# Layer sums accumulated by TensorE through an identity product, and casts of the recurrent mixer moved from VectorE to ScalarE and GpSimd

## The chip, the core and the metric

The kernel runs on one core of one Trainium2 chip. Its engines are TensorE (PE; PEld is its weight load), VectorE (DVE), ScalarE (ACT), GpSimd (POOL) and SyncE (SP), which here only issues DMAs. The metric is the device time of one execution in microseconds (us), as the median of several runs.

## The reference

512 tokens of width 1024 go through two layers. In each layer `x = LN(alpha*x + mixer(x))` and then `x = LN(alpha*x + MoE(x))`. Layer 0 has a convolution mixer, layer 1 a recurrent mixer (RG-LRU). The mixture of experts sends each token to 2 of 16 experts.

```python
def rglru_mixer(x, ...):
    y_branch, xr = split(x @ w_in)
    xr = causal_depthwise_conv(xr, c_dw) + c_dw_b
    r = sigmoid(xh @ w_gate_a + b_gate_a)        # xh: xr in 4 heads of 256
    i = sigmoid(xh @ w_gate_x + b_gate_x)
    log_a = -8 * r * softplus(-lam);  a = exp(log_a)
    b = sqrt(-expm1(2 * log_a)) * (i * xr)
    h = scan(h = a * h + b)                      # over the 512 tokens
    return (gelu(y_branch) * h) @ w_out

def moe(x, ...):
    e_idx, gates = route(x)                      # 2 experts of 16 for each token
    y = expert(x[tokens of e]); out[token] += gate * y

for layer in range(2):
    x = layer_norm(alpha * x + mixer(x), ln1_g, ln1_b)
    f = moe(x, ...)
    x = layer_norm(alpha * x + f, ln2_g, ln2_b)
```

All inputs are float32. The kernel splits an operand of most products into a high part (rounded to the fast float32r form) and a low part (what is left) and makes three products of them: high x high, high x low, low x high.

## The kernel before

Each engine runs its instructions strictly in the order in which the program's text issues them; nothing is reordered, and an instruction that waits holds up all behind it on its engine. So the order of the calls in the Python text is the order of the work.

**Weights.** `Stream` loads pieces of weights by SP's DMA queue, in a planned list. `split` makes the high part `wh` on ACT (line 137) and the low part `wl` by a subtraction on DVE or POOL (line 148, `lower`; `low()` sets which engines take turns). `lead` is how many pieces are split ahead of the one in use. With `later = []` the subtractions are put off and cut into quarters, until `lows()` issues them.

**Layer end.** The last expert's product ends in the sum `alpha*x + MoE(x)`. While the last expert (e = 15) runs, `base_begin` loads, by POOL's DMA queue, four tiles `az` (128 tokens of the layer's input, 128x1024) and `ay` (the two expert rows of each token, gathered in DRAM so far), and POOL adds the two rows (line 1491, in tile order 0 to 3). `base_sum(t)` on DVE makes `az = alpha*az + ay` (line 1496). The last expert's output comes in two column halves: `share(h)` scales it by the gate into `yh` (ACT, line 1502) and `yl` (DVE, 1503), `total_mm` puts its rows at their tokens by products with a 0/1 matrix `place` (PE, 1509), and `total_half` adds that to `az` (DVE, 1516) and takes statistics of the sum (DVE `bn_stats`, 1517), 128x512 at a time, 8 times in a layer. After that `moments` (POOL raises to a power, 549) and the normalisation on ACT (1676 in layer 0, 1768 in layer 1) follow. In the same stretch run the last expert's own steps: `turn` transposes the hidden rows and splits them (`ht0h`, `ht1h` on ACT, 418; `ht0l`, `ht1l` on DVE, 421), and `w2(0)` to `w2(3)` are four groups of 12 products; `w2(1)` needs `ht1l` and `w2(3)` is the second half's last. On DVE four quarters of a put-off subtraction (148, 128x512 each) stand between `ht0l` and `ht1l`.

**Recurrent mixer.** `order1` sets its items: x0 to x7 (projections of 128 channels each, with the convolution), g0 to g3 (gates of two x items each), y0 to y7 (gelu branch), a0, i0, a1, i1 (gate weights), o (rows of w_out). An x item is: 24 products on PE, `xc` (ACT, 994), three steps of the convolution on DVE (997, reading a PSUM bank), then the split `xch` of `xc` into high (DVE cast, 420) and low part (DVE subtraction, 421). A g item is 24 products of `xch`, four sigmoids and two tanh on ACT (973, 977), two square roots (983) and products on POOL (978, 984). `spend` puts pieces of the recurrence between the items on DVE (925, 927, 930 to 932). A y item ends in `gy` (ACT, 1007). `finish(c)` multiplies `gy` by the recurrence's result (DVE, 938) and splits the product into `mixo` (DVE cast 420 and subtraction 421) for the output projection (line 651), which starts after y7. The weight piece of y7 is split by ACT right after the `gy` of y6.

Of the kernel before, what the change touches and what calls it, by code (L numbers as in the profile page):

```python
# [11 lines left out]
F32 = mybir.dt.float32  # L12
# [3 lines left out]
AF = mybir.ActivationFunctionType  # L16
OP = mybir.AluOpType
AX = mybir.AxisListType

P = 128  # L20
T = 512
NT = T // P
# [7 lines left out]
ALPHA = 4.0 ** 0.25  # L30
# [317 lines left out]
class Trunk:  # L348
# [564 lines left out]
    def rglru_mixer(self, xT, first, wa, prm, hook):  # L913
        nc, ws, v, lsc = self.nc, self.ws, self.nc.vector, self.lsc
# [21 lines left out]
        def finish(c):  # L936
            y = ys.pop(c)
            v.tensor_tensor(y, y, hs.pop(c), op=OP.mult)
            m = self.V([P, 2, T], F32R, "mixo")
            self.hilo(m[:, 0], m[:, 1], y, False)  # L940
            self.mixo[c] = m

        credit = [0.0]
# [44 lines left out]
        for pos, item in enumerate(self.order1):  # L988
            kind, n = item[0], int(item[1:] or 0)
            hook(item)  # L990
            if kind == "x":
                ps = first.pop(0) if first else self.project_in(xT, ws.get())
                x = self.W([P, T], F32, "xc")
                nc.scalar.activation(x, ps, AF.Identity, bias=prm[:, n, B_C:B_C + 1],
                                     scale=prm[:, n, W_C + 3:W_C + 4])
                for s in range(1, 4):
                    v.scalar_tensor_tensor(x[:, s:], ps[:, 0:T - s], prm[:, n, W_C + 3 - s:W_C + 4 - s],
                                           x[:, s:], op0=OP.mult, op1=OP.add)
                xc[n] = x
                m = self.V([P, 2, T], F32R, "xch")  # L1000
                self.hilo(m[:, 0], m[:, 1], x, False)
                xch[n] = (m[:, 0], m[:, 1])
                spend(1.5)
            elif kind == "y":
                ps = self.project_in(xT, ws.get())
                y = self.W([P, T], F32, "gy")
                nc.scalar.activation(y, ps, AF.Gelu_apprx_tanh)
                ys[n] = y
                spend(4.0)
            elif kind in "ai":  # L1010
                if item != "a0":
                    wg.setdefault(n, []).append(ws.get())
            elif kind == "g":
                gates(n)
                if n % 2:
                    wg.pop(n // 2)
                spend(3.0)
            else:
                self.out_weights(1)
# [331 lines left out]
    def moe(self, layer, loaded):  # L1351

        nc, tc, ws = self.nc, self.tc, self.ws
# [33 lines left out]
        for e in range(E):  # L1387
            cur, last = nxt, e == E - 1
            if e < 12:
                q = e // 4 * 4 + 4 + 2 * (e % 4)  # L1390
                if e % 4 < 2:
                    hot += [self.one_hot(self.pos[:, :, i], nc.gpsimd, i in SMALL) for i in (q, q + 1)]
                if e % 4 == 2:
                    q = e // 4 * 4 + 4
# [21 lines left out]
                    xe = self.gather(slots[e + 2], e + 2 in SMALL, rows)  # L1416
            ws.later = []
            cur.w3(3)
            cur.turn(0)
            ws.lows()  # L1420
            if last:
# [4 lines left out]
            cur.w2(0)  # L1426
            if last:
                loaded()
                self.base_sum(0)
            cur.w2(1)  # L1430
            if e == E - 2:
                self.place_rows(slots[E - 1][0])
# [12 lines left out]
                    self.kept = None  # L1445
        gate = slots[E - 1][1]
        self.share(0, cur.ys[0], gate)
        for t in (1, 2):
            self.base_sum(t)
        ws.lead = 1  # L1450
        cur.w2(2)
        self.base_sum(3)
        ws.lead = 0
        for t in range(NT):
            self.total_mm(t, 0)
        cur.w2(3)
        for t in range(2):
            self.total_half(t, 0)
        self.share(1, cur.ys[1], gate)
        for t in range(2):  # L1460
            self.total_mm(t, 1)
        for t in range(2, NT):
            self.total_half(t, 0)
            self.total_mm(t, 1)
        ws.total, ws.open, ws.cap = False, False, 10
        ws.lead = 4
        ws.later = []
# [12 lines left out]
    def base_begin(self):  # L1480

        nc = self.nc
        self.bz, self.bp, self.yhl, self.bst = [], {}, {}, {}
        for t in range(NT):
            z = self.V([P, D], F32, "az")
            nc.gpsimd.dma_start(z, self.x1d[t * P:(t + 1) * P])  # L1486
            y = self.V8([P, 2, D], F32, "ay")
            nc.gpsimd.dma_start(y, self.yd[2 * t * P:2 * (t + 1) * P].rearrange("(p k) d -> p k d", k=2))  # L1488
            self.bz.append((z, y))
        for _, y in self.bz:  # L1490
            nc.gpsimd.tensor_tensor(y[:, 0], y[:, 0], y[:, 1], op=OP.add)

    def base_sum(self, t):

# [4 lines left out]
    def share(self, h, ps, gate):  # L1499
# [3 lines left out]
        self.nc.vector.scalar_tensor_tensor(lo, ps, gate, hi.bitcast(F32), op0=OP.mult, op1=OP.subtract)  # L1503
        self.yhl[h] = (hi, lo)

    def total_mm(self, t, h):
        ps = self.bp[t, h] = self.bank()
        for i, q in enumerate(self.yhl[h]):
            self.nc.tensor.matmul(ps, self.place[:, t * P:(t + 1) * P], q, start=(i == 0), stop=(i == 1))  # L1509

    def total_half(self, t, h):

        if h == 0:
            self.bst[t] = self.S([P, 2, 6], F32, "bst", bufs=4)
        z = self.halves(self.bz[t])[h]
        self.nc.vector.tensor_tensor(z, z, self.bp.pop((t, h)), op=OP.add)  # L1516
        self.nc.vector.bn_stats(self.bst[t][:, h], z)  # L1517

    def total(self, t):

        self.total_half(t, 1)
        return self.halves(self.bz[t]), self.moments(self.bst.pop(t))

    def extra(self, layer, it):

# [277 lines left out]
```

## Time and profile before

| | us |
|---|---|
| median of 3 runs (1524.83 to 1527.47) | 1525.57 |
| the profiled execution, its own time | 1530.19 |
| its span, first to last instruction | 1528.4 |
| mixture of experts of layer 0 (215 to 700 us) | 485 |
| layer end 0 (700 to 750) | 50 |
| recurrent mixer up to its last input projection (750 to 895) | 145 |
| its output projection, router (895 to 975) | 80 |
| mixture of experts of layer 1 (975 to 1455) | 480 |
| layer end 1 and the output (1455 to 1528) | 73 |

Times in the trace are from the span's start. A timeline row has the start, the length and the instruction, and in brackets how long its engine had been idle and what ended that. A length runs from the start to the end, waiting for a busy resource included; rows that follow on one engine overlap a little. "x4" is four instructions merged.

### The profile page before, as it was taken

The page shows a single profiled execution, that of the slowest core. Times are in us where ns is not written, and L with a number is a line of the kernel's source. Part 1 is how long each engine was busy: PE and PEld are TensorE (multiplying, and loading weights), DVE is VectorE, ACT ScalarE, POOL GpSimd, SP SyncE. Part 2 cuts the span into 40 slices and gives each one's busy share as a digit, 9 for nine tenths or more (in the row PEclk, how much of TensorE's full clock was granted, in tenths as well). Part 3 has the DMA queues.
Part 4 walks back from the last instruction along what each step waited for, and adds up shares of the span by engine and source line. Part 5 has one row for each costly group of instructions (what it writes and reads, how often), then busy time and mean ns, then how long its engine had stood idle before and what let it go on. Part 6 is the DMA issues. An engine that isn't in the chain of part 4 may idle for free. (4 is left out here: it accounts for less than half of the span.)

```text
span 1528.4 us, 18167 instructions
## 1 busy us (share of the span) xinstructions
PE 1396.3 (91%) x6456; PEld 1026.4 (67%) x6456; DVE 1126.9 (74%) x1242; ACT 772.2 (51%) x718; POOL 432.9 (28%) x370
## 2 busy tenths in 40 slices
PE   8999959999999999999689798699999999999972
PEld 7877738677586775677577677485776858665851
DVE  6997788668484774478989987885866748554886
ACT  3543227466473755376546421373755747554741
POOL 3983015204202400003384312250051015000043
PEclk9999979999999999999799999799999999999995
DMA  9645748999999999988823258399999999999771
GB/s 282 219 193 193 286 186 310 392 419 417 420 415 413 421 414 420 420 355 330 228 70 93 94 206 318 144 365 406 421 419 420 410 416 421 415 420 419 286 311 55
DMA packets 120837, 490.71 MB, mean 321 GB/s; under 512 B 14078, under 2 KB 53502, under 8 KB 70564
## 3 DMA queue, kind: packets, MB, share of 16 engines
q1 hardware_dynamic: 102240, 437.29, 72.6%
q0 software_dynamic: 11808, 35.28, 5.9%
q10 hardware_dynamic: 6692, 16.91, 3.0%
q8 instruction: 53, 0.87, 0.2%
q14 instruction: 44, 0.36, 0.1%
HBM read 469.50 MB, written 29.62 MB: 327 GB/s over the span
## 5 line engine op out<-in xcount | busy, mean ns | idle before, releaser
L148 DVE TENSOR_TENSOR wl<-raw,wh 128x2048 fp32r<-128x2048 f32 (+2 forms) x310 | 630.1, 2075 | 242.0 <-ACT wh L137 210.4
L137 ACT ACTIVATE wh<-raw 128x2048 fp32r<-128x2048 f32 (+1 forms) x312 | 535.2, 1757 | 110.3 <-PE p L305 27.0
L305 PE MATMUL p<-wh,xe 128*128 128x512 f32 x1344 | 347.6, 396 | 1.0 <-PEq L1439 0.8
L305 PEld LDWEIGHTS p<-wh,xe 128*128 128x128 f32 x1344 | 248.8, 189 | 56.9 <-issue 7.0
L305 PE MATMUL p<-wl,xe 128*128 128x512 f32 x672 | 187.9, 391 | 3.5 <-DVE wl L148 3.5
L1346 POOL DMA_INDIRECT yd<-y,io x30 | 30.8, 1026 | 497.1 <-ACT y L1344 199.3
L305 PEld LDWEIGHTS p<-wl,xe 128*128 128x128 f32 x672 | 126.0, 188 | 32.3 <-DVE wl L148 5.2
L226 PE MATMUL b<-raw,xs 128*64 128x512 f32 x640 | 146.2, 598 | 0.0
L1278 POOL TENSOR_SCALAR S<-c,posp 128x128 bf16<-128x128 bf16 x96 | 127.0, 1337 | 0.5
L596 PE MATMUL b<-xT,wh 128*128 128x512 f32 (+1 forms) x320 | 119.2, 379 | 6.0 <-ACT wh L137 6.0
L597 PE MATMUL b<-xT,wh 128*128 128x512 f32 (+1 forms) x320 | 118.5, 377 | 3.0 <-DVE xT L421 3.0
L1331 POOL DMA_INDIRECT xe<-x1d,ii x32 | 37.3, 1167 | 291.9 <-PE b L271 138.4
L226 PEld LDWEIGHTS b<-raw,xs 128*64 128x64 f32 x640 | 42.4, 136 | 75.0 <-issue 69.6
L148 POOL TENSOR_TENSOR wl<-raw,wh 128x1024 fp32r<-128x1024 f32 x28 | 71.3, 2555 | 29.3 <-ACT wh L137 14.9
L599 PE MATMUL b<-xT,wl 128*128 128x512 f32 (+1 forms) x320 | 73.5, 373 | 3.8 <-DVE wl L148 3.8
L596 PEld LDWEIGHTS b<-xT,wh 128*128 128x128 f32 x320 | 62.3, 195 | 17.7 <-ACT wh L137 7.6
L597 PEld LDWEIGHTS b<-xT,wh 128*128 128x128 f32 x320 | 62.2, 194 | 13.8 <-DVE xT L421 3.6
L226 PE MATMUL b<-raw,hts 128*64 128x512 f32 x320 | 70.9, 595 | 0.0
L599 PEld LDWEIGHTS b<-xT,wl 128*128 128x128 f32 x320 | 56.9, 191 | 14.3 <-DVE wl L148 4.2
L1344 ACT ACTIVATE y<-p,sg 128x512 f32<-128x512 f32 x40 | 25.3, 685 | 75.4 <-PE p L305 75.4
L761 DVE SCALAR_TENSOR_TENSOR b<-av,c,b 128x510 f32<-128x510 f32 (+27 forms) x87 | 59.8, 731 | 2.2 <-ACT b L754 1.3
L326 DVE TENSOR_TENSOR hs<-hs,p 128x512 f32<-128x512 f32 x44 | 30.2, 685 | 39.6 <-PE p L305 39.6
(309 smaller groups left out, 1913.4 us busy)
## 6 DMA issues: line engine op xcount, KB each, us to landing
raw<-in_moe_w_dram SPq DMA_DIRECT2D x384, 1024.0 KB, 15.3
raw<-in_even_w_in_dram SPq DMA_DIRECT2D x20, 512.0 KB, 7.5
yd<-zero ACTq DMA_DIRECT2D x8, 1024.0 KB, 5.0
ay<-yd POOLq DMA_DIRECT2D x8, 1024.0 KB, 15.0
raw<-in_odd_w_in_dram SPq DMA_DIRECT2D x16, 512.0 KB, 7.5
raw<-in_even_w_out_dram SPq DMA_DIRECT2D x8, 512.0 KB, 8.5
x1d<-z POOLq DMA_DIRECT2D x8, 512.0 KB, 7.6
az<-x1d POOLq DMA_DIRECT2D x8, 512.0 KB, 12.2
```

The lines of the kernel that those rows point to most:

```text
L137: self.k.nc.scalar.activation(wh, raw, AF.Copy)
L148: self.lo[0].tensor_tensor(wl, raw, wh.bitcast(F32), op=OP.subtract)
L226: self.nc.tensor.matmul(ps[64 * h:64 * h + 64], stat[i], w[0][:, i, h * HALF:(h + 1) * HALF], start=(first and i == 0), stop=(last and i = ...
L305: self.nc.tensor.matmul(pss[j], stat[i][a], q[:, i, j * HALF:(j + 1) * HALF], start=(first and i == 0 and a == 0 and q is wh), stop=(last ...
L326: self.nc.vector.tensor_tensor(self.hm[h], self.hm[h], self.p3[h], op=OP.mult)
L596: nc.tensor.matmul(ps, ah, bh, start=(i == 0), stop=False)
L597: nc.tensor.matmul(ps, ah, bl, start=False, stop=False)
L599: nc.tensor.matmul(ps, al, bh, start=False, stop=(i == n - 1))
L761: nc.vector.scalar_tensor_tensor(o[:, s:], av[:, 0:T - s], prm[:, i, 30 - s:31 - s], acc[:, s:], op0=OP.mult, op1=OP.add)
L1278: (eng or self.nc.vector).tensor_scalar(S[:, t], self.iota2 if small else self.iota, pos[:, t:t + 1], None, op0=OP.is_equal)
L1331: self.nc.gpsimd.indirect_dma_start(out=xe, out_offset=None, in_=self.by_half(self.x1d) if small else self.x1d[:, :], in_offset=bass.Indir ...
L1346: nc.gpsimd.indirect_dma_start(out=self.by_half(self.yd) if small else self.yd[:, :], out_offset=bass.IndirectOffsetOnAxis(ap=slot[2], axi ...
```

## The change

It has two parts.

**Layer end.** `base_begin` only loads. A new `base_add`, called after `w3(3)` of the last expert, scales `az` of tiles 0 and 1 by alpha on ACT, and POOL adds the two rows of each tile and, for tiles 0 and 1, also the scaled `az` to that. DVE keeps `base_sum` for tiles 2 and 3. `base_mm` puts `az` into a PSUM bank by a product with the identity (8 in a layer, both operands float32), `total_mm` adds the last expert's rows into the same bank, and `bn_stats` and the normalisation read the bank. The 8 additions on DVE are gone.

**Recurrent mixer.** The high part of `xch` (8 times) and of `mixo` (8 times) is made on ACT, and the low part of `mixo` on POOL.

```diff
@@ finish
-            self.hilo(m[:, 0], m[:, 1], y, False)
+            nc.scalar.activation(m[:, 0], y, AF.Copy)
+            nc.gpsimd.tensor_tensor(m[:, 1], y, m[:, 0].bitcast(F32), op=OP.subtract)
@@ x items
-                self.hilo(m[:, 0], m[:, 1], x, False)
+                self.hilo(m[:, 0], m[:, 1], x)
@@ moe, last expert
             cur.w3(3)
+            if last:
+                self.base_add()
             cur.turn(0)
...
                 loaded()
-                self.base_sum(0)
             cur.w2(1)
...
         self.share(0, cur.ys[0], gate)
-        for t in (1, 2):
-            self.base_sum(t)
         ws.lead = 1
         cur.w2(2)
+        ws.lead = 0
+        for t in range(2):
+            for h in range(2):
+                self.base_mm(t, h)
+        self.base_sum(2)
+        cur.w2(3)
         self.base_sum(3)
-        ws.lead = 0
-        for t in range(NT):
+        self.base_mm(2, 0)
+        self.base_mm(2, 1)
+        for t in range(3):
             self.total_mm(t, 0)
-        cur.w2(3)
-        for t in range(2):
-            self.total_half(t, 0)
+        self.base_mm(3, 0)
+        self.total_mm(3, 0)
         self.share(1, cur.ys[1], gate)
-        for t in range(2):
-            self.total_mm(t, 1)
-        for t in range(2, NT):
-            self.total_half(t, 0)
-            self.total_mm(t, 1)
+        self.total_mm(0, 1)
+        self.total_mm(1, 1)
+        self.base_mm(3, 1)
+        self.total_mm(2, 1)
+        self.total_mm(3, 1)
@@ new and changed functions
+    def base_add(self):
+        nc = self.nc
+        for z, _ in self.bz[:2]:
+            nc.scalar.activation(z, z, AF.Copy, scale=ALPHA)
+        for t, (z, y) in enumerate(self.bz):
             nc.gpsimd.tensor_tensor(y[:, 0], y[:, 0], y[:, 1], op=OP.add)
+            if t < 2:
+                nc.gpsimd.tensor_tensor(z, z, y[:, 0], op=OP.add)
+                self.bz[t] = z
+    def base_mm(self, t, h):
+        ps = self.bp[t, h] = self.bank()
+        self.nc.tensor.matmul(ps, self.ident, self.halves(self.bz[t])[h], start=True, stop=False)
     def total_mm(self, t, h):
-        ps = self.bp[t, h] = self.bank()
+        ps = self.bp[t, h]
         for i, q in enumerate(self.yhl[h]):
-            self.nc.tensor.matmul(ps, self.place[:, t * P:(t + 1) * P], q, start=(i == 0), stop=(i == 1))
+            self.nc.tensor.matmul(ps, self.place[:, t * P:(t + 1) * P], q, start=False, stop=(i == 1))
-        z = self.halves(self.bz[t])[h]
-        self.nc.vector.tensor_tensor(z, z, self.bp.pop((t, h)), op=OP.add)
-        self.nc.vector.bn_stats(self.bst[t][:, h], z)
+        self.nc.vector.bn_stats(self.bst[t][:, h], ps)
     def total(self, t):
-        self.total_half(t, 1)
-        return self.halves(self.bz[t]), self.moments(self.bst.pop(t))
+        return [self.bp.pop((t, h)) for h in range(2)], self.moments(self.bst.pop(t))
```

POOL at layer end 0, behind the loads, before the change:

```order
L1488 DMA ay_5763<-yd_773 128x2048
L1491 TENSOR_TENSOR ay_5753<-ay_5753 128x1024
L1491 TENSOR_TENSOR ay_5756<-ay_5756 128x1024
L1491 TENSOR_TENSOR ay_5760<-ay_5760 128x1024
L1491 TENSOR_TENSOR ay_5763<-ay_5763 128x1024
```

And with the change:

```order
L1494 DMA ay_5763<-yd_773 128x2048
L1503 TENSOR_TENSOR ay_5753<-ay_5753 128x1024
L1505 TENSOR_TENSOR az_5751<-az_5751,ay_5753 128x1024
L1503 TENSOR_TENSOR ay_5756<-ay_5756 128x1024
L1505 TENSOR_TENSOR az_5751<-az_5751,ay_5756 128x1024
L1503 TENSOR_TENSOR ay_5760<-ay_5760 128x1024
L1503 TENSOR_TENSOR ay_5763<-ay_5763 128x1024
```

POOL has six additions in place of four, and the two new ones stand between the others.

DVE at the same place with the change, from the low parts of the turned rows on:

```order
L421 TENSOR_TENSOR ht0l_5878<-b_5872,ht0h_5877 128x512
L148 TENSOR_TENSOR wl_5845<-raw_5769,wh_5844 128x512 x4
L421 TENSOR_TENSOR ht1l_5891<-b_5885,ht1h_5890 128x512
L148 TENSOR_TENSOR wl_5897<-raw_5793,wh_5896 128x2048
L148 TENSOR_TENSOR wl_5916<-raw_5811,wh_5915 128x2048
L1518 SCALAR_TENSOR_TENSOR yl_5935<-p_5894,sg_4361,yh_5934 128x512
L1511 SCALAR_TENSOR_TENSOR az_5758<-az_5758,ay_5760 128x1024
L1511 SCALAR_TENSOR_TENSOR az_5758<-az_5758,ay_5763 128x1024
```

The four quarters still stand ahead of `ht1l`; of the four sums of 128x1024 two are left, both behind `yl`.

ACT at the end of the mixer's input projections (`gy` of y4 to y7, and `wh` pieces), before the change:

```order
L1007 ACTIVATE gy_6924<-b_6899 128x512
L137 ACTIVATE wh_6936<-raw_6626 128x1024 x2
L1007 ACTIVATE gy_6970<-b_6945 128x512
L137 ACTIVATE wh_6976<-raw_6728 128x1024
L1007 ACTIVATE gy_7005<-b_6980 128x512
L137 ACTIVATE wh_6976<-raw_6728 128x1024
L137 ACTIVATE wh_7019<-raw_6890 128x1024
L1007 ACTIVATE gy_7048<-b_7023 128x512
```

And with the change; the second row of `wh_6978` is the weight piece of y7:

```order
L1008 ACTIVATE gy_6926<-b_6901 128x512
L940 ACTIVATE mixo_6929<-gy_6926 128x512
L137 ACTIVATE wh_6938<-raw_6628 128x1024 x2
L1008 ACTIVATE gy_6972<-b_6947 128x512
L940 ACTIVATE mixo_6929<-gy_6972 128x512
L137 ACTIVATE wh_6978<-raw_6730 128x1024
L1008 ACTIVATE gy_7007<-b_6982 128x512
L940 ACTIVATE mixo_7014<-gy_7007 128x512
L137 ACTIVATE wh_6978<-raw_6730 128x1024
L137 ACTIVATE wh_7021<-raw_6892 128x1024
L1008 ACTIVATE gy_7050<-b_7025 128x512
L940 ACTIVATE mixo_7014<-gy_7050 128x512
```

A cast of `mixo`, which needs DVE's multiplication of line 938, now stands ahead of each weight piece: that of channel block 6 ahead of the piece of y7.

## Rows read from the trace of the kernel before

**Rows 1.** Busy time of each engine by stretch (start:end, length, then busy us and instruction counts of PE, PEld, DVE, ACT, POOL; granted TensorE clock as a share of 2.4 GHz; DMA share; GB/s).

```profile
215.00:700.00 485.00, 479.71 (x2211) 333.66 (x2210) 331.20 (x282) 283.57 (x226) 97.22 (x79) 1.00 0.95 387
700.00:750.00 50.00, 36.91 (x146) 28.03 (x144) 46.10 (x50) 23.07 (x23) 20.02 (x18) 0.87 1.06 349
750.00:895.00 145.00, 122.50 (x548) 100.95 (x549) 135.16 (x133) 75.68 (x99) 74.75 (x39) 0.93 0.25 79
...
1455.00:1528.00 73.00, 34.03 (x127) 25.91 (x125) 54.36 (x57) 20.79 (x20) 31.01 (x24) 0.75 0.45 177
```

**Rows 2.** Timeline of POOL, then of DVE, early in the mixer (start, length, instruction); the last row is the same cast with POOL idle.

```profile
770.24 2.42 POOL L1717 TENSOR_TENSOR n<-n,g 128x1024 f32<-128x1024 f32 x1
772.74 2.46 POOL L1718 TENSOR_TENSOR n<-n,b 128x1024 f32<-128x1024 f32 x1
...
768.32 2.32 DVE L997 SCALAR_TENSOR_TENSOR xc<-b,c,xc 128x511 f32<-128x511 f32 x3 [3.80 <-ACT xc L994]
770.73 2.22 DVE L420 CAST xch<-xc 128x512 fp32r<-128x512 f32 x1
772.99 2.77 DVE L421 TENSOR_TENSOR xch<-xc,xch 128x512 fp32r<-128x512 f32 x1
...
790.96 0.43 DVE L420 CAST xch<-xc 128x512 fp32r<-128x512 f32 x1
```

**Rows 3.** Timeline of layer end 0: POOL's additions, DVE, PE's first product that waits for `yl`, ACT's first normalisation, and POOL's first work of the next stage.

```profile
712.69 2.53 POOL L1491 TENSOR_TENSOR ay<-ay 128x1024 f32<-128x1024 f32 x1 [5.28 <-DMA ay<-yd]
717.95 2.45 POOL L1491 TENSOR_TENSOR ay<-ay 128x1024 f32<-128x1024 f32 x1 [2.73 <-DMA ay<-yd]
...
727.38 2.88 POOL L1491 TENSOR_TENSOR ay<-ay 128x1024 f32<-128x1024 f32 x1 [1.49 <-DMA ay<-yd]
...
715.66 2.49 DVE L148 TENSOR_TENSOR wl<-raw,wh 128x512 fp32r<-128x512 f32 x4
718.06 0.68 DVE L421 TENSOR_TENSOR ht1l<-b,ht1h 128x512 fp32r<-128x512 f32 x1
...
728.76 0.79 PE L1509 MATMUL b<-yl,place 128*128 128x512 f32 x1 [4.71 <-DVE yl L1503]
...
743.39 1.52 ACT L1676 ACTIVATE n<-az,mv 128x512 f32<-128x512 f32 x2 [3.30 <-DVE mv L1673]
...
747.48 9.76 POOL L148 TENSOR_TENSOR wl<-raw,wh 128x1024 fp32r<-128x1024 f32 x4
```

**Rows 4.** Timeline of layer end 1: POOL's additions of tiles 0, 1 and 2, DVE's quarters and `ht1l`, and POOL's first product of the output.

```profile
1467.52 3.69 POOL L1491 TENSOR_TENSOR ay<-ay 128x1024 f32<-128x1024 f32 x1 [4.41 <-DMA ay<-yd]
...
1472.80 2.41 POOL L1491 TENSOR_TENSOR ay<-ay 128x1024 f32<-128x1024 f32 x1 [1.59 <-DMA ay<-yd]
...
1478.60 4.02 POOL L1491 TENSOR_TENSOR ay<-ay 128x1024 f32<-128x1024 f32 x1 [3.38 <-DMA ay<-yd]
...
1472.90 4.67 DVE L148 TENSOR_TENSOR wl<-raw,wh 128x512 fp32r<-128x512 f32 x4
1477.49 0.68 DVE L421 TENSOR_TENSOR ht1l<-b,ht1h 128x512 fp32r<-128x512 f32 x1
...
1506.83 1.34 POOL L1772 TENSOR_TENSOR z<-z,g 128x384 f32<-128x384 f32 x1
```

**Rows 5.** PE's timeline in the first expert: products of two float32 operands, 128x512, merged.

```profile
215.13 15.50 PE L296 MATMUL p<-raw,xf 128*128 128x512 f32 x32
```

**Rows 6.** Costliest groups between 740 and 905 us: DVE's casts and subtractions that the change takes away (count, busy us, mean ns of one, idle before).

```profile
L420 DVE CAST mixo<-gy 128x512 fp32r<-128x512 f32 x7 | 7.1, 1021 | 0.4
...
L420 DVE CAST xch<-xc 128x512 fp32r<-128x512 f32 x8 | 6.7, 836 | 0.5
...
L421 DVE TENSOR_TENSOR mixo<-gy,mixo 128x512 fp32r<-128x512 f32 x7 | 4.8, 692 | 0.2
```

**Rows 7.** Timelines of ACT and POOL in the mixer: two 128x512 ACT instructions from SBUF to SBUF, and one 128x512 two-input POOL instruction.

```profile
790.78 1.16 ACT L983 ACTIVATE sq<-gt 128x512 f32<-128x512 f32 x2
...
789.82 1.29 POOL L978 TENSOR_TENSOR gt<-gt,xc 128x512 f32<-128x512 f32 x1
```

**Rows 8.** PE's waits between 760 and 930 us (total, times, longest), the product after the longest of them, the first sigmoid of g0 on ACT, and DVE's convolution of x2.

```profile
PE b L596 <- DVE xch L420: 10.2, 2, 7.7
...
863.02 0.80 PE L596 MATMUL b<-xch,wh 128*128 128x512 f32 x1 [7.67 <-DVE xch L420]
...
783.26 0.69 ACT L973 ACTIVATE gt<-b,c 128x512 f32<-128x512 f32 x1 [5.33 <-PE b L599]
...
788.62 2.31 DVE L997 SCALAR_TENSOR_TENSOR xc<-b,c,xc 128x511 f32<-128x511 f32 x3
```

**Rows 9.** Timeline at the end of the mixer's input projections: ACT's two weight pieces (y7's first), DVE's multiplications of channel blocks 4, 5 and 6, PE's first product of y7 and the first of the output projection.

```profile
887.78 2.10 ACT L137 ACTIVATE wh<-raw 128x1024 fp32r<-128x1024 f32 x2
...
877.87 2.23 DVE L938 TENSOR_TENSOR gy<-gy,hv 128x512 f32<-128x512 f32 x1 [0.60 <-ACT gy L1007]
...
888.65 0.68 DVE L938 TENSOR_TENSOR gy<-gy,hv 128x512 f32<-128x512 f32 x1
...
897.63 0.69 DVE L938 TENSOR_TENSOR gy<-gy,hv 128x512 f32<-128x512 f32 x1
...
888.88 0.50 PE L596 MATMUL b<-xT,wh 128*128 128x512 f32 x1 [1.69 <-ACT wh L137]
...
894.46 0.62 PE L651 MATMUL b<-wh,mixo 128*128 128x512 f32 x2
```

More of the change, by code (lines that the diff above doesn't have):

```diff
@@ L1489, in base_begin @@
             self.bz.append((z, y))
-        for _, y in self.bz:
+    def base_add(self):
[3 more added lines that the diff above has]
+        for t, (z, y) in enumerate(self.bz):
             nc.gpsimd.tensor_tensor(y[:, 0], y[:, 0], y[:, 1], op=OP.add)
+            if t < 2:
+                nc.gpsimd.tensor_tensor(z, z, y[:, 0], op=OP.add)
+                self.bz[t] = z
     def base_sum(self, t):
@@ L1504, in share @@
         self.yhl[h] = (hi, lo)
+    def base_mm(self, t, h):
+        ps = self.bp[t, h] = self.bank()
+        self.nc.tensor.matmul(ps, self.ident, self.halves(self.bz[t])[h], start=True, stop=False)
     def total_mm(self, t, h):
-        ps = self.bp[t, h] = self.bank()
+        ps = self.bp[t, h]
         for i, q in enumerate(self.yhl[h]):
-            self.nc.tensor.matmul(ps, self.place[:, t * P:(t + 1) * P], q, start=(i == 0), stop=(i == 1))
-    def total_half(self, t, h):
+            self.nc.tensor.matmul(ps, self.place[:, t * P:(t + 1) * P], q, start=False, stop=(i == 1))
         if h == 0:
             self.bst[t] = self.S([P, 2, 6], F32, "bst", bufs=4)
-        z = self.halves(self.bz[t])[h]
-        self.nc.vector.tensor_tensor(z, z, self.bp.pop((t, h)), op=OP.add)
-        self.nc.vector.bn_stats(self.bst[t][:, h], z)
+        self.nc.vector.bn_stats(self.bst[t][:, h], ps)
     def total(self, t):
-        self.total_half(t, 1)
-        return self.halves(self.bz[t]), self.moments(self.bst.pop(t))
+        return [self.bp.pop((t, h)) for h in range(2)], self.moments(self.bst.pop(t))
     def extra(self, layer, it):
```

## The prediction

> **What bounds the kernel now.** I read the busy times by stretch first [rows 1]. From 215 to 700 us PE is busy for 479.71 of 485 us: no edit touches that stretch or its twin in layer 1. What the change touches are three short stretches in which DVE is the fullest engine or close to it: layer end 0 (DVE 46.10 of 50), the recurrent mixer (135.16 of 145, PE 122.50) and layer end 1 (54.36 of 73). ACT and POOL have room there (in the mixer 75.68 and 74.75). Read so, moving work off DVE should pay. But a share of busy time doesn't tell what an instruction does while it is "busy", so I read timelines next.
>
> The first thing to see is a **lock between DVE and POOL**. Early in the mixer POOL runs two operations of 2.42 and 2.46 us [rows 2]. The cast that DVE begins beside the first takes 2.22 us and the subtraction beside the second 2.77; each ends when POOL's operation ends. The same cast takes 0.43 with POOL idle. DVE's convolution, which reads a PSUM bank, runs at its usual 2.32 for three beside POOL. So a DVE cast or subtraction from SBUF waits for the whole POOL operation that runs, and afterwards the next POOL operation waits for DVE: they go by turns. Part of DVE's 135 us is such waiting, and each new POOL operation brings more of it.
>
> The second is the **order at the ends**: in layer end 0, `ht1l` ends at 718.74 behind four quarters, PE's first product of `yl` comes at 728.76 after waiting 4.71 for it, the first normalisation at 743.39, and POOL's lows of the next stage at 747.48 [rows 3]. In the mixer PE loses 10.2 us in two waits for `xch` [rows 8], and y7 starts at 888.88, behind its weight piece on ACT [rows 9].
>
> The sum is made against the profiled execution: 1530.19 us, 1.8 over its span of 1528.4, 4.6 over the median of 1525.57. A difference worked out in the trace is added to the median. A measurement of this kernel can tell some 0.2% (3 us) from no change.
>
> **Layer end 0.** Removed from DVE: two sums of 128x1024 and eight additions of 128x512. Added: two scalings on ACT, two additions on POOL, and eight identity products on PE. Two float32 operands cost 15.50/32 = 0.48 us a product [rows 5], so 3.9 us for eight. The banks are filled while PE waits for `yl` anyway (4.71), so I count nothing; without that cover it would be 3.9.
>
> What is lost comes from POOL. Its first addition ends at 712.69 + 2.53 = 715.22; now five more can follow, at some 2.45 each, the next being the new sum of tile 0. DVE's four quarters stand at 715.66 and took 2.49 together [rows 3], about 0.6 each. Before, they fell into POOL's gap until 717.95. Now they take turns: POOL to 717.65, quarter, POOL to 720.7, quarter, POOL to 723.8, quarter, POOL to 726.4, quarter. `ht1l` starts near 727.1, not 718.06: 9 us later. PE has nothing else then. Later on `yl` no longer waits behind DVE's two sums: the 4.71 that PE waited go. The first normalisation moves by 9.0 - 4.7 = +4.3. Between it and the next stage four of the removed additions (0.68 each, by `ht1l`, of the same size) give back 2.7: **+1.6 us**. Bounds: -4.7 if the quarters slip through as before and `yl`'s wait goes; +4.3 if nothing is given back.
>
> **Layer end 1.** The same replay [rows 4]: POOL's first addition ends at 1471.21, the new sum to 1473.65, then turns with the quarters, which were done at 1477.57 and now end near 1483. `ht1l` starts 5.6 later. Tile 2's rows come late here (POOL's addition at 1478.60 after 3.38 idle, 4.02 long), so there is one turn less. Afterwards DVE's eight additions are gone, 8 x 0.68 = 5.4, from the way to POOL's first product of the output (1506.83). +5.6 - 5.4 = **0**. Bounds: -5.4 if `ht1l` doesn't slip, +5.6 if the additions were hidden.
>
> **Mixer, `xch`.** DVE's eight casts go, 6.7 us [rows 6]. But the low part stays on DVE right behind and needs ACT's result: DVE now waits about 0.7 (a 128x512 on ACT from SBUF takes 1.16/2 = 0.58 [rows 7], and a hand-over 0.1) where an undisturbed cast took 0.43 [rows 2]. So one item loses 0.24 where the cast was free (8 x 0.24 = 1.9 in all), and gains only what the casts waited for POOL: 8 x (0.836 - 0.43) = 3.2. Net 1.3 at best. ACT gets new things to queue: the cast of x2 needs DVE's convolution (788.62 plus 2.31 [rows 8]); a sigmoid of g0 ran at 783.26, and gate work that is issued behind such a cast now waits for it.
>
> **Mixer, `mixo`.** DVE loses 1.021 + 0.692 = 1.71 us a channel block [rows 6]. POOL gains a subtraction of 1.29 each [rows 7], which by the lock can hold up a DVE operation for that long.
>
> **Mixer, the end.** The order on ACT decides it. The weight piece of y7 ran at 887.78, straight after `gy` of y6. Now the cast of `mixo` 6 stands before it, and that needs DVE's multiplication of channel block 6, which ended at 897.63 + 0.69 = 898.32 [rows 9]. If DVE kept its times, y7 would start at 898.32 + 0.6 (cast) + 1.05 (piece, 2.10/2) + 0.1 = 900.1, 11.2 us late. So DVE must be that much earlier for the change to cost nothing here: the multiplication has to end by 887.1.
>
> How much earlier is it? From the end of multiplication 4 (877.87 + 2.23 = 880.10) to that of 6 are 18.2 us, with two channel blocks' casts and low parts in between: 2 x 1.71 = 3.4 saved by the means; 2 x (2.22 + 0.69) = 5.8 if both casts had met POOL. Ahead of multiplication 4: `xch` +1.3 at best, four blocks of `mixo` 4 x 1.71 = 6.8, less up to 4 x 1.29 = 5.2 of the lock; I take a lead of 2, with the ends -1.9 (round trips alone) and +8.1. POOL's low parts of blocks 4 and 5 cost between 0 and 2.6 there; I take 0, since other DVE work reads PSUM or may fall beside. Multiplication 6 ends at 898.3 - 2 - 3.4 = 892.9 and y7 starts at 894.7: **+5.8**. Ends: 898.3 + 1.9 - 3.4 + 2.6 gives y7 at 901.2, +12.3; with 8.1 and 5.8 the multiplication would be at 884.4 and no longer the limit: y7 could gain about 1 (its wait for the piece) and what PE recovers of its 10.2 us of waits [rows 8], of which I allow 3: -4.
>
> **The clock.** y7 now comes after about 6 us without work. After 7.67 idle a product took 0.80 [rows 8], where y7's 24 took (894.46 - 888.88)/24 = 0.23 each. If a third of them run at twice 0.23, 8 x 0.23 = **+1.9**; bounds 0 and 24 x 0.23 = 5.5. The output projection follows directly (894.46 [rows 9]), and PE is its bound, so what y7 loses is lost.
>
> The Trainium skill ("Perfetto Trace Analysis", section "Optimizing Scalar/DVE Operations") warns that GpSimd and DVE share an SBUF read port, so that moving operations between those two might not help. The trace agrees, with 2.22 for 0.43 us; by that rule alone the two additions and `mixo`'s low part on POOL give nothing.
>
> **Sum.** 1.6 + 0 + 5.8 + 1.9 = +9.3 us: 1525.57 + 9.3 = 1534.9.
>
> **The rivals.** *Relief (faster).* DVE is nearly full in all three stretches [rows 1] and loses 18.6 us in the mixer [rows 6]. If POOL's additions come before or after the quarters, not between them, layer end 0 gives -4.7 and layer end 1 -5.4; if multiplication 6 ends by 887.1, the mixer is at 0 to -4. That is 1525.6 - 10.1 = 1515.5, down to 1511.5, and 1520 or so where one of the two ends fails. For it: 93% busy means that freed time moves the next step forward. Against it: DVE must be 11.2 us earlier at multiplication 6, and the largest lead with the blocks' mean, 8.1 + 3.4 = 11.5, just does that if POOL's new operations hold up nothing; with 2.6 of the lock it is 8.9. The point from which it decides is 887.1. The same section of the Trainium skill says that with DVE saturated, moving work to ScalarE or even GpSimd may make sense; this is that case, as far as 135.16 of 145 is saturation. Chance 0.27.
>
> *Cancelled (same).* Multiplication 6 ends at about 889 and y7 loses 2, the ends give 2 back: 1525.6. It also holds the case that the change at the layer ends is hidden: PE's waits there swap places only. Chance 0.15.
>
> *More lock (slower still).* Each new POOL operation holds DVE, and the sigmoids wait behind the casts for g0, g1 and g2: 1525.6 + 12.3 (y7 at its bound) + 1.9 (clock) + 4.3 (layer end 0 at its bound) = 1544. Chance 0.08.
>
> **How the numbers follow.** My own case has 0.50. Slower by over 0.2%: 0.50 x 0.95 + 0.08 + a little, 0.57; within 0.2% 0.16; faster 0.27. The range reaches up to the worse rival's 1544, with some 0.06 beyond, and down to 1516, so that it holds the upper part of the relief and leaves out about 0.12. Of my own case alone: 1529 to 1541.
>
> **What would show it.** In the trace after: (1) POOL's six additions and DVE's quarters by turns in layer end 0, `ht1l` near 727 (wrong if under 720); (2) PE's wait for `yl` at 728 gone; (3) first normalisation near 747.5; (4) in layer end 1 `ht1l` near 1483, less what the stages before shifted; (5) multiplication 6 at 893 and y7's first product at 894.7, waiting for ACT's weight piece, with the granted clock down in that stretch; (6) g0's first sigmoid later than 783.3. The forecast is wrong if y7 starts before 890 or `ht1l` keeps its times; the relief is then at work.

## The result: slower by 1.3%

Median 1548.26 us (1541.94 to 1548.63, 3 runs) against 1525.57: ratio 1.0133, 95% interval 1.011 to 1.0156, 22.7 us. The forecast of slower was right; its size, +9.3, was too small and the time lies above the range. The profiled execution of the changed kernel has a span of 1547.0 us, 18.6 over that of before; the ledger below adds up to that. (The other 4 us lie between the profiled executions and the medians: before's profile was 4.6 above its median, this one 0.4 above its own.) Two things make the ledger's share of the layer ends rather too small. Counted from PE's first turn of the last expert, which came at 711.99 here and at 713.63 before, layer end 0 takes 4.3 us longer and not 2.6. And this profile of the kernel before has long ends: from that first turn to the ledger's row the two ends together take 80.8 us in it, 78.0 to 79.7 in the seven experiments below that leave the ends as they were, and 88.2 with the change.

| from the traces, before and after | start before | start after | later by | added here | forecast |
|---|---|---|---|---|---|
| POOL's first low of the mixer (end 0 is over) | 747.48 | 750.11 | 2.6 | 2.6 | 1.6 |
| PE's first product of y7 | 888.88 | 902.31 | 13.4 | 10.8 | 5.8 |
| DVE's first sum of the output projection | 921.18 | 936.45 | 15.3 | 1.8 | 1.9 |
| PE's first turn of the last expert, layer 1 | 1470.99 | 1486.46 | 15.5 | 0.2 | 0 |
| POOL's last product of the output | 1517.97 | 1536.56 | 18.6 | 3.1 | 0 |

The stretch of the mixer in the busy times of the changed kernel (columns as in [rows 1]):

```profile
750.00:895.00 145.00, 120.02 (x538) 97.77 (x537) 120.61 (x113) 81.43 (x113) 81.14 (x45) 0.92 0.23 75
```

DVE has fallen from 135.16 to 120.61 [rows 1], just as meant, and y7 comes 10.8 us later behind the mixer's start. Who waits for whom between 760 and 930 us in the changed kernel (total, times, longest):

```profile
ACT mixo L940 <- DVE gy L938: 21.4, 8, 6.1
...
PE b L596 <- ACT wh L137: 14.9, 5, 8.5
...
PE b L596 <- ACT xch L418: 11.0, 3, 8.2
...
DVE xch L421 <- ACT xch L418: 6.2, 8, 0.8
```

PE's waits for `xch` are still there, 11.0 for 10.2 [rows 8], and those for weight pieces on ACT have grown from 2.0 to 14.9. The timeline at y7, ACT, then DVE's multiplications of blocks 4 and 6, then PE; it answers to [rows 9]:

```profile
894.54 0.63 ACT L940 ACTIVATE mixo<-gy 128x512 fp32r<-128x512 f32 x1 [6.10 <-DVE gy L938]
...
900.68 0.63 ACT L940 ACTIVATE mixo<-gy 128x512 fp32r<-128x512 f32 x1 [4.08 <-DVE gy L938]
901.22 1.99 ACT L137 ACTIVATE wh<-raw 128x1024 fp32r<-128x1024 f32 x2
...
883.19 2.21 DVE L938 TENSOR_TENSOR gy<-gy,hv 128x512 f32<-128x512 f32 x1 [0.59 <-ACT gy L1008]
...
899.90 0.69 DVE L938 TENSOR_TENSOR gy<-gy,hv 128x512 f32<-128x512 f32 x1
...
902.31 0.79 PE L596 MATMUL b<-xT,wh 128*128 128x512 f32 x1 [8.52 <-ACT wh L137]
```

Read from below: PE stands 8.52 for the piece; ACT starts the piece right behind the cast; the cast had waited 4.08 for a multiplication that ends at 900.59. y7 follows it by 1.72 us. The clock granted to TensorE stood at 1.2 GHz when y7's products began, after those 8.52 us without work, and rose to 2.4 GHz within them: 0.73 of full speed on average, 1.00 before, and the 24 products take 7.42 us for 5.58.

Early in the mixer, ACT and DVE in the changed kernel, answering to the sigmoid of 783.26 in [rows 8]:

```profile
791.39 0.63 ACT L418 ACTIVATE xch<-xc 128x512 fp32r<-128x512 f32 x1 [9.61 <-POOL n L1733]
...
793.33 1.27 ACT L974 ACTIVATE gt<-b,c 128x512 f32<-128x512 f32 x2
...
798.96 0.43 DVE L925 TENSOR_SCALAR gt<-gt 128x512 f32<-128x512 f32 x1 [6.21 <-ACT sq L984]
```

ACT idles 9.61 us before the cast of x2, g0's sigmoid comes 10.1 us later than before (2.6 of them are the mixer's later start), and DVE then has nothing to do for 6.21: the relieved engine waits for work that the move itself has delayed.

Layer end 0, timelines of POOL, DVE and PE, answering to [rows 3]:

```profile
713.65 2.37 POOL L1505 TENSOR_TENSOR az<-az,ay 128x1024 f32<-128x1024 f32 x1
716.45 2.37 POOL L1503 TENSOR_TENSOR ay<-ay 128x1024 f32<-128x1024 f32 x1 [0.43 <-DMA ay<-yd]
718.90 2.70 POOL L1505 TENSOR_TENSOR az<-az,ay 128x1024 f32<-128x1024 f32 x1
721.57 2.78 POOL L1503 TENSOR_TENSOR ay<-ay 128x1024 f32<-128x1024 f32 x1
...
715.33 9.57 DVE L148 TENSOR_TENSOR wl<-raw,wh 128x512 fp32r<-128x512 f32 x4
724.82 0.68 DVE L421 TENSOR_TENSOR ht1l<-b,ht1h 128x512 fp32r<-128x512 f32 x1
...
725.55 2.08 PE L305 MATMUL p<-wh,ht1l 128*128 128x512 f32 x4 [5.28 <-DVE ht1l L421]
```

The four quarters take 9.57 us for 2.49, one to each POOL operation. In layer end 1 it is 10.69 for 4.67 [rows 4]; there DVE and PE read on like this:

```profile
1488.69 10.69 DVE L148 TENSOR_TENSOR wl<-raw,wh 128x512 fp32r<-128x512 f32 x4
...
1506.49 0.74 DVE L1518 SCALAR_TENSOR_TENSOR yl<-p,sg,yh 128x512 fp32r<-128x512 f32 x1
...
1514.94 1.89 DVE L1533 BATCH_NORM_STATS2 bst<-b 128x6 f32<-128x512 f32 x3 [5.44 <-PE b L1530]
...
1517.81 0.73 DVE L1518 SCALAR_TENSOR_TENSOR yl<-p,sg,yh 128x512 fp32r<-128x512 f32 x1
...
1500.03 2.07 PE L305 MATMUL p<-wh,ht1l 128*128 128x512 f32 x4 [8.01 <-DVE ht1l L421]
...
1506.38 3.59 PE L1524 MATMUL b<-az,c 128*128 128x512 f32 x8
...
1518.60 0.50 PE L1530 MATMUL b<-yl,place 128*128 128x512 f32 x1 [1.21 <-DVE yl L1518]
```

Before, PE waited here for the first half's `yl`:

```profile
1488.77 0.79 PE L1509 MATMUL b<-yl,place 128*128 128x512 f32 x1 [5.49 <-DVE yl L1503]
```

The second half's `yl` comes 11.3 us behind the first's (8.96 before, 1487.97 to 1496.93): it stands on DVE behind statistics that wait 5.44 us for PE. PE itself waits only 1.21 us for it. But the 5.49 us that PE has won are filled with identity products: from the end of `ht1l` to the last product of the sums PE takes 21.4 us, 21.5 before, and in layer end 0 21.2 for 20.3. The identity products, in the costliest groups of the whole kernel (count, busy, mean ns):

```profile
L1524 PE MATMUL b<-az,c 128*128 128x512 f32 x32 | 15.0, 592 | 0.0
```

There are 16 such products in two layers, but 32 records: a product of two float32 operands is two records, 15.0/16 = 0.94 us each. I had divided [rows 5] by its records.

### The profile page after: what moved, and what is told of

Same layout as the page of the kernel before. It is cut to its first block, busy times and chain, and to the rows that moved or that the text cites. A ratio compares the mean times of both kernels' runs of the same rounds, so it can differ in the third digit from the quotient of the medians.

```text
span 1547.0 us, 18204 instructions
## 1 busy us (share of the span) xinstructions
PE 1411.3 (91%) x6488; PEld 1032.5 (67%) x6488; DVE 1103.7 (71%) x1198; ACT 783.0 (51%) x738; POOL 452.3 (29%) x382
## 5 line engine op out<-in xcount | busy, mean ns | idle before, releaser
L148 DVE TENSOR_TENSOR wl<-raw,wh 128x2048 fp32r<-128x2048 f32 (+2 forms) x310 | 642.8, 2116 | 256.7 <-ACT wh L137 234.8
L596 PE MATMUL b<-xT,wh 128*128 128x512 f32 (+1 forms) x320 | 121.5, 386 | 18.9 <-ACT wh L137 18.9
L597 PE MATMUL b<-xT,wh 128*128 128x512 f32 (+1 forms) x320 | 120.1, 382 | 2.6 <-DVE xT L421 2.6
L305 PE MATMUL p<-wh,ht1l 128*128 128x512 f32 x176 | 49.1, 402 | 13.3 <-DVE ht1l L421 13.3
```

The costliest lines, as they stand in the source:

```text
L148: self.lo[0].tensor_tensor(wl, raw, wh.bitcast(F32), op=OP.subtract)
L305: self.nc.tensor.matmul(pss[j], stat[i][a], q[:, i, j * HALF:(j + 1) * HALF], start=(first and i == 0 and a == 0 and q is wh), stop=(last ...
L596: nc.tensor.matmul(ps, ah, bh, start=(i == 0), stop=False)
L597: nc.tensor.matmul(ps, ah, bl, start=False, stop=False)
```

## The experiments

All times are beside runs of the kernel before on the same chip, in three groups of four. Theory A: what is lost is order; an instruction put on an engine's queue holds what stands behind it (a cast on ACT that waits for DVE, additions on POOL that go by turns with DVE). The rivals are named in the expectations.

**Each part alone.** The ends as changed, with the mixer of before:

```diff
-            nc.scalar.activation(m[:, 0], y, AF.Copy)
-            nc.gpsimd.tensor_tensor(m[:, 1], y, m[:, 0].bitcast(F32), op=OP.subtract)
+            self.hilo(m[:, 0], m[:, 1], y, False)
...
-                self.hilo(m[:, 0], m[:, 1], x)
+                self.hilo(m[:, 0], m[:, 1], x, False)
```

> Only the layer ends are changed; the recurrent mixer is as before. Theory A (each part costs by itself; in the trace of the changed kernel layer end 0 came out 2.6 us later and layer end 1 some 2 to 3 us): +5 us, 1530.5; ht1l some 6 us later in both ends because POOL's additions and DVE's quarters go by turns. Theory B (the ends are neutral and all of the loss is the mixer): within 2 us of 1525.6.

Measured 1531.79 against 1524.73, +7.1, ratio 1.0064 (1.0042 to 1.0085); counted from PE's first turn, `ht1l` is 6.4 and 6.3 us later than before, as expected. Then the reverse edit of the kernel before, the whole mixer:

> Only the recurrent mixer is changed. Theory A: y7 starts about 11 us late (its weight piece on ACT behind the cast of mixo 6) and the output projection starts with a low clock, +13 to +15 us, 1539 to 1541. Theory B: +18 us, 1544. If the parts add, the loss here and that of the layer ends alone make up the whole.

1537.26, +12.5, 1.0101 (1.0069 to 1.0132). The two add to 19.6 of 22.7, within their intervals: both parts lose. y7 starts at 898.45, 1.73 behind the end of multiplication 6 (896.72). The expected +13 to +15 was near. The stretches in the traces agree with the times: from POOL's first low to the first product of the output projection the mixer takes 160.1 us here and 147.0 before, and the two ends take 86.0 us in the run with the ends alone (78.0 to 80.8 unchanged). Then the mixer's two halves:

> Only the eight casts of xch on ACT. Theory A (a cast on ACT that waits for DVE's convolution holds the sigmoids of the gates behind it): g0's first sigmoid near 791 instead of 783.3, the recurrence's first step near 796 instead of 792, +2 to +3 us at the end, 1528. Theory C (DVE is relieved of 6.7 us and that counts): -3 us, 1522.6.

1531.42, +6.7, 1.0053 (1.003 to 1.0076): twice to three times the expected loss. g0's sigmoid came at 788.74, not 791, since the mixer began 1.5 us earlier here (POOL's first low at 745.98). The worst place is g2: the cast of x6 and the sigmoids, on ACT:

```profile
847.33 0.63 ACT L418 ACTIVATE xch<-xc 128x512 fp32r<-128x512 f32 x1 [9.31 <-DVE xc L997]
847.98 1.28 ACT L973 ACT_TABLE_LOAD   x1
849.28 1.27 ACT L973 ACTIVATE gt<-b,c 128x512 f32<-128x512 f32 x2
```

Before, the first of these sigmoids ran at 833.63. The load of ACT's function table in the second row is not new: there are 15 such loads in the traces of both kernels and of every run. Multiplication 6 ends at 903.67, 5.4 later than before although the mixer began 1.5 earlier: 6.9 us lost on DVE's chain.

> Only the casts of mixo on ACT and their low parts on POOL. Theory A (order on ACT): y7's first product starts 1.7 us after DVE's multiplication of channel block 6 ends, near 895 instead of 888.9, and 2 us more by the clock, +7 us, 1532.6. Theory C (DVE relieved by 1.7 us a channel block): y7 at or before 890, -1 to +1 us.

1532.48, +7.8, 1.0056 (1.0029 to 1.0083). Multiplication, cast, weight piece and y7, on DVE, ACT and PE:

```profile
889.58 0.69 DVE L938 TENSOR_TENSOR gy<-gy,hv 128x512 f32<-128x512 f32 x1
...
890.37 0.63 ACT L940 ACTIVATE mixo<-gy 128x512 fp32r<-128x512 f32 x1 [4.08 <-DVE gy L938]
890.90 1.99 ACT L137 ACTIVATE wh<-raw 128x1024 fp32r<-128x1024 f32 x2
...
892.00 0.79 PE L596 MATMUL b<-xT,wh 128*128 128x512 f32 x1 [8.53 <-ACT wh L137]
```

DVE's multiplication ends at 890.27, 8.1 earlier than before (6.9 from the mixer's start): here the relief is real. But it had to be 11.2, and y7 again follows by 1.73. So `mixo` gives DVE's chain 6.9 us and `xch` takes 6.9 away; together multiplication 6 stands where it was (896.72 + 1.4 of earlier start, 898.1 against 898.3), and y7 pays the whole delay.

**The same work in another order.** If the queue is the cause, the same instructions on the same engines must cost nothing elsewhere in it. First, `mixo`'s cast is put off until the next item's own ACT work has been issued:

```diff
-            nc.scalar.activation(m[:, 0], y, AF.Copy)
-            nc.gpsimd.tensor_tensor(m[:, 1], y, m[:, 0].bitcast(F32), op=OP.subtract)
+            late.append((m, y))
...
                 nc.scalar.activation(y, ps, AF.Gelu_apprx_tanh)
                 ys[n] = y
+                flush()
```

> The casts of mixo on ACT and the low parts on POOL as in the run with mixo alone, but each cast is issued after the next item's own ACT work, so that the weight piece of y7 stands ahead of the cast of block 6. Same engines, same instructions, another order on ACT. Theory A (order): y7's first product no longer follows the multiplication of block 6; PE's wait of 8.5 us is 2 or less; +7 us goes, 1521 to 1525 beside 1524.7 of before. Theory B (POOL's low parts hold DVE by the lock, or the casts load ACT): stays at 1530 to 1533.

1526.52 against 1524.69, +1.8, 1.0012 (1.0001 to 1.0024). Six of the 7.8 us are gone; the expectation's upper end was missed by 1.5, and PE's wait is 3.7 where 2 or less was expected. The same thing happens one block earlier, ACT and PE:

```profile
885.29 0.63 ACT L946 ACTIVATE mixo<-gy 128x512 fp32r<-128x512 f32 x1 [1.40 <-DVE gy L938]
885.83 1.99 ACT L137 ACTIVATE wh<-raw 128x1024 fp32r<-128x1024 f32 x2
...
886.92 0.80 PE L596 MATMUL b<-xT,wh 128*128 128x512 f32 x1 [3.73 <-ACT wh L137]
```

Counted from POOL's first low y7 is not late here (141.0 us, 141.4 before). What is left of the loss is the clock after that wait: 0.64 of full speed over y7's 24 products, which take 8.45 us for 5.58.

Next, `xch`'s casts of x2, x4 and x6 behind the gates that follow them:

```diff
+                if self.order1[pos + 1][0] == "g":
+                    after.append((m, x))
+                else:
+                    self.hilo(m[:, 0], m[:, 1], x)
```

> The casts of xch on ACT as in the run with xch alone, but those of x2, x4 and x6 are issued after the gates' sigmoids. Theory A (a cast waiting for DVE's convolution holds the sigmoids): sigmoids of g1 and g2 at their times before (807 and 834, not 818 and 849), y7 near 889, 1523 to 1527. Theory D (the round trip from DVE to ACT and back costs in each x item, whatever the order): y7 stays near 894, 1530.

1527.57, +2.9, 1.0018 (1.0006 to 1.0031). The sigmoids are back at 807.72 and 834.89, y7 at 889.74; counted from the mixer's start, which was 1.8 us earlier here, the sigmoids are still 2.3 and 3.0 us late (12 and 17 with all casts ahead of the gates) and y7 2.6. About 4 of the 6.7 us were the held sigmoids (theory A). The rest fits theory D, but isn't shown to be it: the low parts on DVE wait for ACT's casts six times in this run, 4.6 us in all, where DVE had casts of 6.7 us [rows 6].

> The whole change of the mixer with both orders mended; layer ends as before. Theory A: the 12.5 us of the mixer go, 1520 to 1525. Theory B or D: 1531 to 1537.

1532.46, +7.8, 1.0054 (1.0031 to 1.0077): theory A's time was missed, and the time lies in the rivals' range. The trace still has A's mechanism. With `xch` on ACT the lead of DVE is gone, multiplication 5 ends at 890.30, and y7's piece, which in this order stands behind the cast of block 5, starts behind it; y7 comes at 891.97 after 3.77 of waiting. Putting the cast off by one item isn't enough, so the last step, again with `mixo` alone, puts off those of blocks 4 to 7 until gelu of y7 (`if n not in (5, 6): flush()`):

> Mixer: casts of mixo on ACT, low parts on POOL, those of blocks 4 to 7 issued only behind gelu of y7, so that no weight piece of y5 to y7 stands behind a cast. In the run with casts one item later y7's piece still stood behind the cast of block 5 (multiplication 5 ended at 885.3, y7 at 886.9 after 3.7 us of waiting). Theory A: that wait goes, y7 near 885, 1521 to 1523, a little faster than before. Rival (DVE's relief reaches nothing that PE waits for, and the casts are late for the output projection): 1525 to 1528.

1524.09 against 1525.50, 0.999 (0.9976 to 1.0003). The whole loss of `mixo` is gone, with all its casts on ACT and low parts on POOL. On ACT and PE y7's piece now follows gelu of y6 directly, and PE's wait is that of [rows 9]:

```profile
883.84 2.00 ACT L137 ACTIVATE wh<-raw 128x1024 fp32r<-128x1024 f32 x2
...
884.94 0.50 PE L596 MATMUL b<-xT,wh 128*128 128x512 f32 x1 [1.69 <-ACT wh L137]
```

y7 came at 884.94, as theory A had it; the time lies between the two ranges named. So neither POOL's low parts nor ACT's load cost anything that PE sees (theory B falls). The relief of DVE gives little: the middle is -1.4 us, within the noise. In the trace the stretch from POOL's first low to the output projection is 143.7 us, against 145.6 to 147.0 in the five traces with the mixer of before, so a gain of 2 to 3 us is likely there, but the times don't show it. `xch` with its casts on ACT was not brought to no loss in any run.

**The layer ends.** Sums of all tiles back on DVE, bank accumulation and PE's order as in the change:

```diff
-        for z, _ in self.bz[:2]:
-            nc.scalar.activation(z, z, AF.Copy, scale=ALPHA)
...
-            if t < 2:
-                nc.gpsimd.tensor_tensor(z, z, y[:, 0], op=OP.add)
...
+                self.base_sum(0)
```

> Only the layer ends: sums in PE's banks by the identity product as in the change, but alpha*x + rows of all four tiles is made on DVE again, nothing new on ACT and POOL. Theory A (POOL's two new additions alternate with DVE's quarters and delay ht1l): ht1l ends near 718 and 1478, the +7 us go, 1521 to 1526. Theory E (the identity products and the later statistics cost): stays at 1529 to 1532 with ht1l early.

1533.11, +8.4, 1.0056 (1.0037 to 1.0075). Theory A for the ends, as the expectation has it, fell: `ht1l` is on time (716.10 and 1474.54) and the loss stays. DVE, then PE, in layer end 1, and last PE's row in layer end 0:

```profile
1482.84 0.74 DVE L1514 SCALAR_TENSOR_TENSOR yl<-p,sg,yh 128x512 fp32r<-128x512 f32 x1
1483.51 4.97 DVE L1507 SCALAR_TENSOR_TENSOR az<-az,ay 128x1024 f32<-128x1024 f32 x3
1494.90 1.89 DVE L1529 BATCH_NORM_STATS2 bst<-b 128x6 f32<-128x512 f32 x3 [6.42 <-PE b L1526]
...
1497.75 0.73 DVE L1514 SCALAR_TENSOR_TENSOR yl<-p,sg,yh 128x512 fp32r<-128x512 f32 x1
...
1486.26 3.24 PE L1520 MATMUL b<-az,c 128*128 128x512 f32 x4 [2.82 <-DVE az L1507]
...
729.42 3.50 PE L1520 MATMUL b<-az,c 128*128 128x512 f32 x4 [5.65 <-DVE az L1507]
```

The identity products of tile 1 now wait 2.82 us (5.65 in layer end 0) for DVE's sum and hold `w2(3)`; in the changed kernel POOL has that sum ready, and PE doesn't wait there. So this run has exchanged one wait for another. Also all products of the first half stand behind `w2(3)`, DVE idles 6.42 us, and the second `yl` is 14.9 us behind the first. So a new theory F: PE's order. The products of `place` open the banks ahead of `w2(3)`, as before the change, the identity products close them behind it, and `yl` is issued ahead of the first statistics:

```diff
+        for t in range(NT):
+            self.rows_mm(t, 0)
         cur.w2(3)
         self.share(1, cur.ys[1], gate)
+        for t in range(NT):
+            self.base_mm(t, 0)
+        for t in range(NT):
+            self.rows_mm(t, 1)
+            self.base_mm(t, 1)
```

> Layer ends only, sums of all four tiles on DVE (as in the run where nothing new is on ACT and POOL), but PE's order is turned round: the products of the first column half stand ahead of w2(3) as before the change and open the banks, the identity products follow behind w2(3) and close them, and yl of the second half is issued ahead of the first half's statistics. Theory F (the loss at the ends is the order: yl of the second half waits on DVE behind statistics that wait for PE): yl of the second half 8 to 9 us behind the first one's instead of 14.9, the +8.4 us go, 1520 to 1525. Theory E (identity products cost wherever they stand): 1529 to 1533.

1526.45 against 1525.50, 1.001 (0.9994 to 1.0027): 7.5 of the 8.4 us are gone, and `yl` is 7.7 behind. The edit turns the order on PE and that of `yl` and the last sums on DVE at once; their shares are not told apart. It is no faster than before, though 5.4 us of DVE's additions a layer are gone, and DVE's and PE's rows say why:

```profile
1491.40 0.70 DVE L1522 BATCH_NORM_STATS2 bst<-b 128x6 f32<-128x512 f32 x1 [0.63 <-PE b L1519]
1492.72 0.70 DVE L1522 BATCH_NORM_STATS2 bst<-b 128x6 f32<-128x512 f32 x1 [0.62 <-PE b L1519]
...
1490.34 1.02 PE L1519 MATMUL b<-az,c 128*128 128x512 f32 x2
```

And DVE's additions of the second half before the change:

```profile
1497.59 0.68 DVE L1516 TENSOR_TENSOR az<-az,b 128x512 f32<-128x512 f32 x1
...
1498.92 0.67 DVE L1516 TENSOR_TENSOR az<-az,b 128x512 f32<-128x512 f32 x1
```

Each tile of the second half now takes 1.32 us, by PE (two products and the identity); before, DVE's addition and statistics took 1.33 from one tile to the next. One engine's step was swapped for another's of equal length. The ends as a whole say the same: what follows PE's last product is 5.1 and 3.3 us shorter than before, and PE's way from `ht1l` to that product 4.4 and 1.9 longer.

> The same order on PE, but tiles 0 and 1 are scaled on ACT and summed on POOL as in the change. What differs from the run before it is the price of POOL's two additions alone. Theory A (by turns with DVE's quarters, ht1l 6 us late): 3 to 5 us more than the run with DVE's sums. Theory G (the turns are hidden): the same within 1.5 us.

1534.98, +9.5, 1.0059 (1.0042 to 1.0077): 8.5 us more than with DVE's sums, where 3 to 5 were expected. Here the turns are bare, DVE and PE in layer end 1:

```profile
1477.13 10.17 DVE L148 TENSOR_TENSOR wl<-raw,wh 128x512 fp32r<-128x512 f32 x4
1487.22 0.68 DVE L421 TENSOR_TENSOR ht1l<-b,ht1h 128x512 fp32r<-128x512 f32 x1
...
1487.95 2.07 PE L305 MATMUL p<-wh,ht1l 128*128 128x512 f32 x4 [7.47 <-DVE ht1l L421]
```

`ht1l` comes 6.4 and 6.2 us later behind PE's first turn than in the run before. Not all of that is POOL: 1.5 and 0.7 us are lost ahead of the quarters, where ACT's scaling of tile 1 waits for its data and holds `ht0h` behind it.

So what the changed kernel loses at its ends is the order on POOL and ACT: without the additions and scalings 8.5 us go, in an order of PE's that costs nothing by itself. PE's order is not shown to be a second cause there. With the additions in place the change's own order costs 7.1 and the turned one 9.5, and the 8.4 of the run with DVE's sums come with a wait that the changed kernel doesn't have.

> Layer ends of g1_rows_first and mixer of g3_mixo_last together, the candidate that should beat both kernels if theories A and F hold: 1517 to 1523. If they don't: 1528 or more.

1526.93, 1.0005 (0.9988 to 1.0023). The expected gain isn't there; the time lies between the two ranges named. This version keeps two pieces of the change, the sums in the banks and the moves of `mixo`; the casts of `xch`, POOL's two additions and ACT's scalings are left out. In a good order these two pieces cost nothing measurable and bring nothing measurable. The pieces left out cost 2.9 us at best (`xch`) and 8.5 (additions and scalings) in the orders tried, and no version here beats the kernel before.

## Why the prediction was right in direction and short in size

By the ledger the forecast of +9.3 is short by another 9.3 us: 5.0 at y7, 3.1 in layer end 1 and 1.0 in layer end 0 are most of it. The other 4 are the distance of before's profiled execution from its median.

- **The lock and the turns: right.** `ht1l` of layer end 0 was forecast near 727 and came at 724.82 (the end began 1.6 us earlier here; the replay's last step slips by 0.4, since 723.8 + 0.6 + 2.45 is 726.9); in layer end 1 near 1483 plus the shift of 15.5, measured 1499.30. The first normalisation came at 748.77, forecast 747.5.
- **y7 behind multiplication 6: right.** 1.75 us forecast, 1.72 measured, and 1.73 in two experiments. Between multiplications 4 and 6 the saving was 18.2 - 15.2 = 3.0, forecast 3.4. The clock: 1.8 us, forecast 1.9, and the first product of y7 took 0.79, as after other long waits (0.50 before). That it came so close is partly luck: the four experiments in which y7's first product is as slow lost 2.2 to 2.9 us there. That y7's delay is the queue on ACT is shown by the pair with and without the cast ahead of it (+7.8 and -1.4).
- **The lead of 2 ahead of multiplication 4: wrong, the step that failed.** I took 2 us earlier, with -1.9 as the worst; measured it ended at 885.40 for 880.10, 5.3 later, of which 2.6 came with the mixer's start: 2.7 late. My own terms gave 2.9 to 8.1 (1.3 + 6.8, less up to 5.2 of the lock); the 2 has no working. The term that failed is `xch`, "net 1.3 at best". I named the sigmoids that queue behind the casts and gave them no price. Alone, counted from POOL's first low, `xch` made multiplication 4 6.8 us later, and 4.2 of these went when the sigmoids stood ahead of the casts again. `mixo` alone made it 3.9 earlier, inside the 6.8 less the lock. The two make 2.9 late.
- **What the ends give back: wrong.** I let `yl`'s wait (4.7) and four additions (2.7) vanish in end 0 and eight (5.4) in end 1, and counted nothing for the identity products, since they would fit into that wait. The wait went, but the products filled it: of the 8.4 and 6.3 us by which `ht1l` slipped, 4.1 and 3.2 came back, not 7.4 and 5.4. End 0 was +4.3 counted from its first turn where I had 1.6, end 1 +3.1 where I had 0. I read what DVE loses and not what it now waits for.
- **The identity product: mis-sized by two.** 0.94 us, not 0.48: 7.5 us of PE a layer where I had 3.9 and a cover of 4.7. The Trainium skill ("FP8 and Floating Point Precision", section "TensorE Precision Notes") says that true FP32 takes four passes through the array; the trace agrees, 0.94 against 0.23 for a product of the fast form is 4.1.
- **The rivals.** Relief was real on DVE for `mixo` (8.1 us earlier) and still did not reach 887.1. "More lock" (1544, chance 0.08) came nearest, and half of its mechanism was at work: the sigmoids did wait behind the casts, y7 came 10.8 us later where its bound was 12.3, and layer end 0 stood at its bound of 4.3. The other half, new POOL operations that hold DVE, showed at the layer ends, where my own case had it too, but not in the mixer: POOL's low parts of `mixo` cost nothing once the casts stood elsewhere.

Open: why `xch` keeps 2.9 us with the sigmoids in order was put down to its low parts' waits by their sum, not by an experiment. Each difference was measured on one chip, but the three groups ran on three chips, so that a comparison between groups (+7.8 and -1.4 for `mixo`) sets differences side by side and not times; the last 3 of 22.7 us between the sum of the parts and the whole are inside the intervals.

## What to carry to other kernels

With engines that run strictly in order, an operation moved to an idle engine isn't free there: its inputs' latest time becomes the earliest time of everything queued behind it. So price a move by what stands behind the new instruction and when its operand is ready, above all weight pieces and gates that PE waits for; then place it in the queue, which here was worth 9 us with not one instruction changed. And check in the place that ends last whether the new engine's step is any shorter: at the layer ends DVE's 1.33 us a tile became PE's 1.32.

## What was not expected of the hardware

- Four DVE quarters of about 0.6 us took 9.57 and 10.69 us in the changed kernel beside a closed row of POOL additions, in layer end 0 of 2.4 to 2.8 us each: turns, one DVE operation to one of POOL. Where POOL had gaps before the change, they took 2.49 and 4.67 us.
- A product of two float32 operands appears as two records in the trace; counted per product it is 0.94 us at a granted clock of 2.4 GHz.
